# RoPE on one core: a zero word from each of 128 partitions between loads 0 and 1, and batch 0 stored whole

## The chip, the cores and the metric

The kernel runs on one core of a Trainium2 chip. Times are device microseconds of one launch; the time of a kernel is the median over its runs. A separate profiled execution gives the trace; its span is the time from the first to the last thing that the profile sees on the core.

## The reference

The input `x` has 8 batches of 2048 positions, 16 heads and 64 values, in float32. Each head's 64 values are two halves of 32, which are rotated by the position's 32 cosines and sines:

```python
out1 = x1 * cos - x2 * sin
out2 = x1 * sin + x2 * cos
return np.concatenate([out1, out2], axis=-1).astype(np.float32)
```

`x` and the output are 67.1 MB each, 8.39 MB a batch. There is no matrix product; three elementwise passes per batch are all of the arithmetic.

## The kernel before

**Tiling.** A batch has 2048 positions; partition p of the 128 holds positions 16p to 16p + 15, so a batch is 16 rows of 1024 values (J = 16) per partition, and a partition's share is one contiguous run of 64 KiB in `x` and in the output. On the chip the values are float16: `buf` (L47) holds NBUF = 5 batches, and batch b uses slot b mod 5, so batches 5, 6 and 7 reuse the slots of 0, 1 and 2.

**Transfers.** `load` (L62 to L71) and `store` (L73 to L81) issue one DMA each, from GpSimd. The transfer itself turns float32 into float16 on the way in and back on the way out. One DMA of a whole batch has 128 packets, one per partition, and 16 short completion packets of 4 bytes; a DMA of two batches has 256 and 16. All of these transfers stand in one queue, which is called the ring here: `in_ring` (L51 to L60) binds each one behind the one issued before it, so that GpSimd issues them in the order of the program and the queue serves them in that order.

SyncE issues four transfers on another queue: `sin_f` (L40), `head` (L41, the first two rows of batch 0 in float32, JA = 2), `cos_f` (L45), and at the end the last two rows of batch 7 (L135), which go out behind the ring's transfer called `gate` (L130).

**Compute.** `rotate` (L83 to L100) makes three VectorE passes over a batch: `v` = the swapped halves times the signed sines (L92), `buf` times the cosines in place (L98), and the sum in place (L100). ScalarE prepares the float16 tables (L104, L105, L110), turns `head` into float16 (L106), and turns the last two rows back (L134).

**Order.** Batch 0 is rotated in two parts, rows 0 and 1 (L111) and rows 2 to 15 (L115). The ring has, in order: load 0 without its first two rows (L102), load 1 (L103), the one-row store of batch 0 (L112), loads 2 and 3 in one DMA (L113), load 4 (L114), the other 15 rows of store 0 (L116), store 1, store 2, loads 5 and 6 (L121), load 7 (L122), stores 3 and 4 (L125), stores 5 and 6 (L128), and store 7 in two parts of 9 and 5 rows (L130, L131). The two-batch loads wait for the slots that they write over: L121 for stores 0 and 1, L122 for store 2. Loads 2 to 4 write slots that nothing has used; they wait for nothing but their place behind the one-row store, which waits for L111 and so for the cosines.

The constants that the program's start sets on GpSimd (zero and one in float32, and two others) are 128 x 1 tiles; the kernel before uses none of them in a transfer.

Of the kernel before, what the change touches and what calls it, by code (L numbers as in the profile page):

```python
# [1 line left out]

# [4 lines left out]


@with_exitstack  # L10
def kernel(
    ctx: ExitStack,
    tc: tile.TileContext,
    x: bass.AP,
    cos: bass.AP,
    sin: bass.AP,
    out: bass.AP,
):
    nc = tc.nc
    f16 = mybir.dt.float16  # L20
    f32 = mybir.dt.float32

    B, S, H, D = x.shape
    Dh = D // 2
    P = nc.NUM_PARTITIONS
    J = S // P
    NBUF = 5

    const_pool = ctx.enter_context(tc.tile_pool(name="rope_const", bufs=1))
    io_pool = ctx.enter_context(tc.tile_pool(name="rope_io", bufs=1))  # L30
    tmp_pool = ctx.enter_context(tc.tile_pool(name="rope_tmp", bufs=1))

    JA = 2
    head = const_pool.tile([P, JA, H, D], f32)
    x0 = x[0].rearrange("(p j) h d -> p j (h d)", j=J)
    sin_f = const_pool.tile([P, J, Dh], f32)
    cos_f = const_pool.tile([P, J, Dh], f32)
    cos_h = const_pool.tile([P, J, Dh], f16)
    sin_h = const_pool.tile([P, J, D], f16)
    nc.sync.dma_start(out=sin_f, in_=sin.rearrange("(p j) d -> p j d", j=J))  # L40
    nc.sync.dma_start(  # L41
        out=head.rearrange("p j h d -> p (j h d)"),
        in_=x0[:, 0:JA, :].rearrange("p j f -> p (j f)"),
    )
    nc.sync.dma_start(out=cos_f, in_=cos.rearrange("(p j) d -> p j d", j=J))  # L45

    buf = io_pool.tile([P, NBUF, J, H, D], f16)  # L47

    ring = []

    def in_ring(dma):  # L51
        if ring:
            tc.add_manual_dep(
                dma.ins,
                ring[-1].ins.name,
                mybir.DependencyInfo(mybir.DependencyClass.NoSync, mybir.DependencyReason.DATA),
                reason="order of the ring",
            )
        ring.append(dma)
        return dma  # L60

    def load(b, n=1):  # L62
        k = b % NBUF
        if n == 1:
            j0 = JA if b == 0 else 0
            dst = buf[:, k, j0:J, :, :].rearrange("p j h d -> p (j h d)")
            src = x[b].rearrange("(p j) h d -> p j (h d)", j=J)[:, j0:J, :].rearrange("p j f -> p (j f)")
        else:
            dst = buf[:, k : k + n, :, :, :].rearrange("p b j h d -> p b (j h d)")
            src = x[b : b + n].rearrange("b (p j) h d -> p b (j h d)", j=J)  # L70
        in_ring(nc.gpsimd.dma_start(out=dst, in_=src))  # L71

    def store(b, n=1, j0=0, j1=J):  # L73
        k = b % NBUF
        if n == 1:
            src = buf[:, k, j0:j1, :, :].rearrange("p j h d -> p (j h d)")
            dst = out[b].rearrange("(p j) h d -> p j (h d)", j=J)[:, j0:j1, :].rearrange("p j f -> p (j f)")
        else:
            src = buf[:, k : k + n, :, :, :].rearrange("p b j h d -> p b (j h d)")
            dst = out[b : b + n].rearrange("b (p j) h d -> p b (j h d)", j=J)  # L80
        return in_ring(nc.gpsimd.dma_start(out=dst, in_=src))  # L81

    def rotate(b, j0=0, j1=J):  # L83
        v = tmp_pool.tile([P, J, H, D], f16)
        n = j1 - j0
        js = slice(j0, j1)
        xt = buf[:, b % NBUF, js, :, :]
        shape = [P, n, H, 2, Dh]
        sin_b = sin_h[:, js, :].rearrange("p j (e d) -> p j e d", e=2).unsqueeze(2).to_broadcast(shape)
        cos_b = cos_h[:, js, :].unsqueeze(2).to_broadcast([P, n, 2 * H, Dh])  # L90
        xe = xt.rearrange("p j h (e d) -> p j h e d", e=2)
        nc.vector.tensor_mul(  # L92
            out=v[:, js, :, :].rearrange("p j h (e d) -> p j h e d", e=2),
            in0=xe[:, :, :, ::-1, :],
            in1=sin_b,
        )
        xw = xt.rearrange("p j h (e d) -> p j (h e) d", d=Dh)
        nc.vector.tensor_mul(out=xw, in0=xw, in1=cos_b)  # L98
        xa = xt.rearrange("p j h d -> p (j h d)")
        nc.vector.tensor_add(out=xa, in0=xa, in1=v[:, js, :, :].rearrange("p j h d -> p (j h d)"))  # L100

    load(0)  # L102
    load(1)  # L103
    nc.scalar.copy(out=sin_h[:, :, Dh:D], in_=sin_f)  # L104
    nc.scalar.mul(out=sin_h[:, :, 0:Dh], in_=sin_f, mul=-1.0)  # L105
    nc.scalar.copy(  # L106
        out=buf[:, 0, 0:JA, :, :].rearrange("p j h d -> p (j h d)"),
        in_=head.rearrange("p j h d -> p (j h d)"),
    )
    nc.scalar.copy(out=cos_h, in_=cos_f)  # L110
    rotate(0, 0, JA)  # L111
    store(0, 1, 0, 1)  # L112
    load(2, 2)  # L113
    load(4)  # L114
    rotate(0, JA, J)  # L115
    store(0, 1, 1, J)  # L116
    rotate(1)
    store(1)
    rotate(2)
    store(2)  # L120
    load(5, 2)  # L121
    load(7)  # L122
    rotate(3)
    rotate(4)
    store(3, 2)  # L125
    rotate(5)
    rotate(6)
    store(5, 2)  # L128
    rotate(7)
    gate = store(7, 1, 0, 9)  # L130
    store(7, 1, 9, J - JA)  # L131
    last = buf[:, 7 % NBUF, J - JA : J, :, :].rearrange("p j h d -> p (j h d)")
    dst = out[B - 1].rearrange("(p j) h d -> p j (h d)", j=J)[:, J - JA : J, :].rearrange("p j f -> p (j f)")
    nc.scalar.copy(out=head.rearrange("p j h d -> p (j h d)"), in_=last)  # L134
    end = nc.sync.dma_start(out=dst, in_=head.rearrange("p j h d -> p (j h d)"))  # L135
    tc.add_manual_dep(
        end.ins,
        gate.ins.name,
        mybir.DependencyInfo(mybir.DependencyClass.Sync, mybir.DependencyReason.DATA),
        reason="the last rows go out behind this part",  # L140
    )


# [1 line left out]
_INS = ['x', 'cos', 'sin']  # L145
_OUTS = [((8, 2048, 16, 64), 'float32')]


# [23 lines left out]
```

## Time and profile before

| what | us |
|---|---|
| median of 3 runs | 316.79 (316.6 to 317.02) |
| the profiled execution | 316.6 |
| its span | 314.8 |
| VectorE busy | 209.1 |
| one VectorE pass over a whole batch (7 of each line) | 8.69 |
| one VectorE pass over rows 2 to 15, over rows 0 and 1 | 7.63, 1.23 |
| GpSimd's issue of one transfer, mean of the stores | 0.586 |
| VectorE's wait for ScalarE's cosines (L98 for L110) | 15.5 |
| VectorE's wait for loads (L92), two times in all | 41.2 |
| GpSimd's wait for stores that free a slot (L71), two times in all | 48.9 |
| HBM read and written | 67.63 MB and 67.11 MB |

The page counts 3104 packets: 2528 on the ring's queue, which is 18 batch-wide parts of 128 rows and 14 sets of 16 completion packets, and 576 on SyncE's queue. Its rate in GB/s counts the bytes as they are written, so a stretch of loads (float16 on arrival) reads near 200 and a stretch of stores near 400 at the same pace of the engines. An engine's idle time is put down to what released it: what the page calls an unknown queue in the chain of waits is a landing that the chain doesn't follow further. Beside the page the trace keeps one record for each packet, with its queue, start, duration and bytes.

### The profile page before, as it was taken

The page shows a single profiled execution, that of the slowest core. Times are in us where ns is not written, and L with a number is a line of the kernel's source. Part 1 is how long each engine was busy: PE and PEld are TensorE (multiplying, and loading weights), DVE is VectorE, ACT ScalarE, POOL GpSimd, SP SyncE. Part 2 cuts the span into 40 slices and gives each one's busy share as a digit, 9 for nine tenths or more (in the row PEclk, how much of TensorE's full clock was granted, in tenths as well). Part 3 has the DMA queues.
Part 4 walks back from the last instruction along what each step waited for, and adds up shares of the span by engine and source line. Part 5 has one row for each costly group of instructions (what it writes and reads, how often), then busy time and mean ns, then how long its engine had stood idle before and what let it go on. Part 6 is the DMA issues. An engine that isn't in the chain of part 4 may idle for free.

```text
span 314.8 us, 115 instructions
## 1 busy us (share of the span) xinstructions
DVE 209.1 (66%) x27; ACT 6.8 (2%) x6; POOL 8.6 (3%) x18
## 2 busy tenths in 40 slices
DVE  0105999999499999999950000899999999910000
ACT  3200000000000000000000000000000000020000
POOL 1002000000000000000010000000000000010000
DMA  9899999999999899999999999999999999999998
GB/s 284 187 262 200 200 266 200 200 262 204 200 200 317 382 492 407 400 400 533 400 200 208 258 200 200 229 237 333 400 491 441 400 400 525 408 400 400 433 427 339
DMA packets 3104, 101.71 MB, mean 323 GB/s; under 512 B 288, under 2 KB 288, under 8 KB 672
## 3 DMA queue, kind: packets, MB, share of 16 engines
q0 software_dynamic: 2528, 99.09, 98.1%
q1 hardware_dynamic: 576, 2.62, 2.2%
HBM read 67.63 MB, written 67.11 MB: 428 GB/s over the span
## 4 chain that ended last, share of the span: by engine, by line
DVE 66%; another core or an unknown queue 13%; DMA 8%; ACT 1%; issue 0%; SPq 0%; DVEq 0%; ACTq 0%
DVE buf L98 22%; DVE buf L100 22%; DVE v L92 22%; DMA cos_f<-in_cos_dram 8%; ACT head L134 1%; ACT cos_h L110 0%; SPq L41 0%; SPq L40 0%; DVEq L92 0%; ACTq L134 0%
## 5 line engine op out<-in xcount | busy, mean ns | idle before, releaser
L92 DVE TENSOR_TENSOR v<-buf,sin_h 128x16384 f16<-128x16384 f16 (+2 forms) x9 | 69.7, 7744 | 51.4 <-DMA buf<-in_x_dram 41.2
L98 DVE TENSOR_TENSOR buf<-buf,cos_h 128x16384 f16<-128x16384 f16 (+2 forms) x9 | 69.7, 7744 | 15.8 <-ACT cos_h L110 15.5
L100 DVE TENSOR_TENSOR buf<-buf,v 128x16384 f16<-128x16384 f16 (+2 forms) x9 | 69.7, 7744 | 0.3
L81 POOL DMA_DIRECT2D out_dram<-buf x8 | 4.7, 586 | 219.4 <-DVE buf L100 219.4
L134 ACT CAST head<-buf 128x2048 f32<-128x2048 f16 x1 | 1.9, 1898 | 249.9 <-DVE buf L100 249.9
L71 POOL DMA_DIRECT2D buf<-in_x_dram x6 | 3.7, 628 | 49.7 <-DMA out_dram<-buf 48.9
L106 ACT CAST buf<-head 128x2048 f16<-128x2048 f32 x1 | 1.9, 1897 | 3.5 <-DMA head<-in_x_dram 3.5
L104 ACT ACT_TABLE_LOAD x1 | 1.3, 1283 | 0.7 <-PEq L156 0.7
L110 ACT CAST cos_h<-cos_f 128x512 f16<-128x512 f32 x1 | 0.6, 617 | 16.1 <-DMA cos_f<-in_cos_dram 16.1
L104 ACT CAST sin_h<-sin_f 128x512 f16<-128x512 f32 x1 | 0.6, 617 | 1.4 <-DMA sin_f<-in_sin_dram 1.4
L105 ACT ACTIVATE sin_h<-sin_f 128x512 f16<-128x512 f32 x1 | 0.6, 624 | 0.0
L156 POOL MEMSET const-float32-0.0<- 128x1 f32 x1 | 0.1, 100 | 0.2 <-issue 0.2
L156 POOL MEMSET const-bfloat16-1.0<- 128x1 bf16 x1 | 0.1, 103 | 0.0
L156 POOL MEMSET const-float32-1.0<- 128x1 f32 x1 | 0.1, 100 | 0.0
L156 POOL MEMSET const-uint8-127<- 128x1 uint8 x1 | 0.1, 100 | 0.0
## 6 DMA issues: line engine op xcount, KB each, us to landing
buf<-in_x_dram POOLq DMA_DIRECT2D x2, 8192.0 KB, 55.2
buf<-in_x_dram POOLq DMA_DIRECT2D x3, 4096.0 KB, 57.4
out_dram<-buf POOLq DMA_DIRECT2D x1, 7680.0 KB, 68.3
out_dram<-buf POOLq DMA_DIRECT2D x1, 4608.0 KB, 28.6
buf<-in_x_dram POOLq DMA_DIRECT2D x1, 3584.0 KB, 22.3
out_dram<-buf POOLq DMA_DIRECT2D x1, 2560.0 KB, 34.1
head<-in_x_dram SPq DMA_DIRECT2D x1, 1024.0 KB, 6.9
out_dram<-head SPq DMA_DIRECT2D x1, 1024.0 KB, 8.4
```

Of the source, the lines that this page charges most:

```text
L71: in_ring(nc.gpsimd.dma_start(out=dst, in_=src))
L81: return in_ring(nc.gpsimd.dma_start(out=dst, in_=src))
L92: nc.vector.tensor_mul(out=v[:, js, :, :].rearrange("p j h (e d) -> p j h e d", e=2), in0=xe[:, :, :, ::-1, :], in1=sin_b,)
L98: nc.vector.tensor_mul(out=xw, in0=xw, in1=cos_b)
L100: nc.vector.tensor_add(out=xa, in0=xa, in1=v[:, js, :, :].rearrange("p j h d -> p (j h d)"))
L104: nc.scalar.copy(out=sin_h[:, :, Dh:D], in_=sin_f)
L105: nc.scalar.mul(out=sin_h[:, :, 0:Dh], in_=sin_f, mul=-1.0)
L106: nc.scalar.copy(out=buf[:, 0, 0:JA, :, :].rearrange("p j h d -> p (j h d)"), in_=head.rearrange("p j h d -> p (j h d)"),)
L110: nc.scalar.copy(out=cos_h, in_=cos_f)
L134: nc.scalar.copy(out=head.rearrange("p j h d -> p (j h d)"), in_=last)
L156: nc = _bacc.Bacc("TRN2", target_bir_lowering=False, num_devices=1)
```

## The change

The one-row store of batch 0 goes. In its place, a DMA on the same queue and in the same order rule writes one float32 zero from each of 128 partitions of the constant tile to the first word of each partition's share of batch 0's output, 64 KiB apart; it stands between load 0 and load 1. Loads 2 to 4 are issued right behind load 1, ahead of the tables and the first rotation. Batch 0 is still rotated in two parts, and then stored in one DMA of 16 rows, which writes the zero words over.

```diff
     load(0)
+    first = out[0].rearrange("(p j) h d -> p (j h d)", j=J)[0:128, 0:1]
+    in_ring(nc.gpsimd.dma_start(out=first, in_=nc.const_aps.tensor(0.0, [128, 1], f32), allow_slow_non_contiguous=True))
     load(1)
+    load(2, 2)
+    load(4)
     nc.scalar.copy(out=sin_h[:, :, Dh:D], in_=sin_f)
...
     rotate(0, 0, JA)
-    store(0, 1, 0, 1)
-    load(2, 2)
-    load(4)
     rotate(0, JA, J)
-    store(0, 1, 1, J)
+    store(0)
     rotate(1)
     store(1)
```

## The prediction

> **What bounds the kernel now.** I read the page's summary by slices and by queues first, then the chain of waits, then the timeline of the queue that issues the transfers, then the issues with their landing times, and last the trace's record of each single DMA packet (queue, start, duration, bytes).
>
> ```profile
> DVE 209.1 (66%) x27; ACT 6.8 (2%) x6; POOL 8.6 (3%) x18
> DMA  9899999999999899999999999999999999999998
> q0 software_dynamic: 2528, 99.09, 98.1%
> ```
>
> The 16 DMA engines are busy in every slice, and q0, the queue that GpSimd fills (the ring), alone takes 98.1% of their time. DVE is busy for two thirds. The chain of waits still puts 66% on DVE:
>
> ```profile
> 78.40 4.89 another core or an unknown queue
> ...
> 161.88 36.10 another core or an unknown queue
> ...
> 276.66 1.90 ACT head L134
> ```
>
> That chain ends at 278.6 us, 36 us before the span does, and inside it DVE stands still for 4.89 and 36.10 us, each time until a load lands. So what ends last is the ring, not DVE. The timeline of GpSimd's queue shows how far ahead the ring is filled:
>
> ```profile
> 1.24 1.21 POOL L71 DMA_DIRECT2D buf<-in_x_dram  x2 [0.80 <-PEq L167]
> 29.53 0.54 POOL L81 DMA_DIRECT2D out_dram<-buf  x1 [27.08 <-DVE buf L100]
> 30.06 1.26 POOL L71 DMA_DIRECT2D buf<-in_x_dram  x2
> 52.52 0.54 POOL L81 DMA_DIRECT2D out_dram<-buf  x1 [21.19 <-DVE buf L100]
> 140.72 0.71 POOL L71 DMA_DIRECT2D buf<-in_x_dram  x1 [30.36 <-DMA out_dram<-buf]
> 159.97 0.56 POOL L71 DMA_DIRECT2D buf<-in_x_dram  x1 [18.54 <-DMA out_dram<-buf]
> 276.88 1.08 POOL L81 DMA_DIRECT2D out_dram<-buf  x2 [25.46 <-DVE buf L100]
> ```
>
> Against it I set the packet records, which give when each transfer's first packet starts on the first of the engines: load 0 5.28, load 1 22.97, the one-row store 42.71, loads 2 and 3 43.95, load 4 82.58, the rest of store 0 101.90, store 1 120.01, store 2 139.33, loads 5 and 6 158.64, load 7 197.27, stores 3 and 4 216.59, stores 5 and 6 255.20, the two parts of store 7 293.81 and 304.69, the last two rows 310.72. Each was issued long before its turn: the nearest misses are 13 us (issued 29.53, turn at 42.71), 18 us (140.72 for 158.64) and 17 us (276.88 for 293.81). No transfer ever waits for its issue, so the time is the sum of what the ring's transfers take, with 5.3 us ahead and 4 us behind.
>
> The records also give the price of a batch: a packet is one partition's row, each engine has eight of them, and they start 2.413 us apart (2.412 for stores): load 4 lasts 82.577 to 101.900 = 19.323 us, store 1 19.315. Only two stretches up to store 0 depart from that price. Load 1 lasts 22.966 to 42.705 = 19.739, that is **0.416 us above** load 4; its eighth packets took 2.74 to 2.90 us where the others took 2.43, right ahead of the first store of the program. And the one-row store (42.705 to 43.950 = 1.245) with the rest (101.900 to 120.011 = 18.111) make 19.356, **0.041 us above** one whole store.
>
> **The change, part by part.** All 16 batches' worth of rows still go through the same ring, so only these small terms can move.
>
> *The one-row store goes, store 0 leaves whole.* 19.356 becomes 19.315: -0.04 us. The ring has 14 transfers before and after (one store less, one word store more), so the 16 four-byte completion packets of a transfer (some 0.02 us per engine) cancel between them; I count the word store's +0.02 with its own price and the split's inside the 0.04.
>
> *Loads 2 to 4 move up by one store.* GpSimd issues them at about 3 to 4 us instead of at 30.06; their rows stand in the ring 38.6 + 19.3 us long wherever the one-row store is. Nothing runs dry either way (13 us of cover now). The ring then holds six transfers at once, 48 data packets per engine, where the trace shows 40 at most (at 162 us: loads 5 to 7 and stores 3 and 4). If it took fewer, GpSimd would wait with load 4 until load 0 had drained at 23.5 us; load 4's turn is at 82 us, and store 0 is not ready before about 50 us, so this costs nothing. Load 1 is issued one DMA instruction later, 1.91 + 0.54 = 2.45 us, for a turn at 22.97.
>
> *The wait that is added.* Store 0 writes the words again that the word store has written, so it waits for that landing, at about 24 us; it is issued near 50 us. Behind it on GpSimd stand store 1 and all later issues; none is delayed.
>
> *cos.* The other queue's transfers share the engines with the ring:
>
> ```profile
> sin_f<-in_sin_dram SPq DMA_DIRECT2D x1, 256.0 KB, 2.7
> cos_f<-in_cos_dram SPq DMA_DIRECT2D x1, 256.0 KB, 24.4
> out_dram<-buf POOLq DMA_DIRECT2D x1, 512.0 KB, 15.2
> ```
>
> cos's packets alternate with load 0's, and on 13 engines its last record comes behind load 1's first row, so it lands at 26.08. With short words there instead, it can land near 23.6, and DVE's first batch ends up to 2.4 us earlier. Worth nothing at the end: DVE then waits for load 2, 4.89 us now, and longer. Without that cover a late DVE would have 13 to 18 us of issue lead to use up first.
>
> *The word store's own price.* Each engine gets eight rows of 4 bytes, from a constant that the program has set at 0.24 us anyway, and a completion packet. No row of the trace writes 4 bytes to memory. From below: the cheapest 4-byte completion records take 0.009 us, so 8 x 0.009 = 0.07. From above: the first rows of sin, 2048 bytes met cold, took mostly 0.404 us where they were slow, so 8 x 0.404 = 3.2 us. Nearest in kind are the 4-byte records inside a stretch of stores, 0.042 us each: 8 x 0.042 = 0.34. The 2048-byte rows in flow, 0.081 us with some 0.075 of it for the bytes, also speak for the lower half. A gain from the words by themselves is excluded: they take ring time. I take 0.34 + 0.02 = +0.36.
>
> The Trainium skill, "DMA: Bandwidth & Descriptors" (section Specifications), speaks against small words: line rate needs 512 bytes or more, and below that an engine reads, modifies and writes. No store of before is that short (its shortest row has 4096 bytes), so no run here shows it yet; by the row above the sum below is +0.32 us, by that rule it is the third rival's +3.2.
>
> *The 0.416 us.* It is a stall at the turn from the first loads to the first store. No later turn from load to store has it (load 4 to store 0: the last packet took 2.432, load 7 to stores 3 and 4 the same). Either the first store of a program pays it, and then the word store pays it between loads 0 and 1 (0 net), or the short 4 KB rows caused it, and it goes (-0.416) or the shorter words cause it too (0). Worst, both the words and the first whole store pay: +0.416. I take 0: it moves.
>
> Sum: -0.04 + 0.36 + 0 = **+0.32 us**. The profiled execution took 316.6 (span 314.8, 1.8 around it), so such a one would take 316.9; the median of the runs, 316.79, is 0.19 above it, which gives **317.1**. A measurement of this kernel can tell about 0.2%, 0.63 us, from no change: the forecast is no change that can be told.
>
> **The rivals.**
> 1. *The stall goes with the 4 KB rows.* For it: its only place is ahead of them. Against: the first store is the same place. 317.1 - 0.42 = 316.7; with the cheapest words (0.07 for 0.34) 316.4. Still within 0.2%.
> 2. *Both turns stall.* For it: nothing but that the word store may be too short to clear whatever the first store meets. 317.1 + 0.42 = 317.5, just over the bound.
> 3. *The words go one at a time, each a round trip to memory* (the other side). Place: between loads 0 and 1 on every engine, so all of the ring behind moves. Price 8 x 0.404 + 0.02 - 0.04 = +3.2 us: 320.0. It decides from the point where a word costs more than (0.63 + 0.04 - 0.02) / 8 = 0.081 us, the price of a 2048-byte row in flow. For it: rows at the start of the kernel did wait 0.35 to 0.64 us each. Against: once the queue flowed, rows overlapped, and behind each store's completion packets the next transfer's rows begin 0.02 us later. The rule in the Trainium skill ("DMA: Bandwidth & Descriptors", Specifications) would amount to this.
> 4. *Doesn't do what it says: the words aren't spread.* All 128 on one engine, 128 x 0.042 = 5.4 us, and that engine ends last: 322. Against: the rows of every transfer in the trace start in sixteens, eight times per batch.
> 5. *Faster beyond the bound.* Load 1's start is also ragged: 22.966 comes 2.349 us after load 0's eighth packet where seven others came 2.204 apart, some 0.13 too much. If stall, split and raggedness all went and the words cost the least: -0.42 - 0.04 - 0.13 + 0.09 = -0.50, 316.3. It needs more that I don't see to pass 0.63.
>
> **How the numbers follow.** Forecast 0.45; rival 1 0.20, rival 2 0.08, rival 3 0.20, rival 4 0.03, rival 5 0.04. Faster by over 0.2%: rival 5 and a tail of rival 1, 0.04 + 0.03 = 0.07. Slower: most of rival 3 (0.18), 0.05 of rival 2, rival 4 = 0.26. Within: 0.67. The range goes from 316.3 (rivals 1 and 5) to 318.6, a word price of (318.6 - 316.79 + 0.02) / 8 = 0.23 us, about the middle of rival 3; left out are some 0.06 below, 0.10 of rival 3 and 0.03 of rival 4 above. The forecast's own range is 316.8 to 317.5.
>
> **What would show it.** In the changed profile: q0 still near 98% and no slice without DMA; load 1's first full rows some 0.4 us of words plus a stall after load 0's end; load 1 itself at 19.32 and load 4 to store 0 without a stall (if the stall is moved); cos landing near 24 us; 19.3 us for store 0; the chain with a longer wait for load 2. It is wrong if the ring shows a gap, if the words take over 0.65 us in all, or if the 2.41 us between rows changes anywhere.

## The result, and the profile after

The changed kernel takes 317.25 us (median of 15 runs, 317.06 to 317.78), the kernel before in the same sessions 316.62 (15 runs, 316.31 to 317.02): a ratio of 1.0022, with a 95% interval of 1.0015 to 1.0029. It is slower by 0.6 us. The profiled span goes from 314.836 to 315.579 us, +0.74.

The page of the changed kernel, the lines that answer to those shown of before:

```profile
span 315.6 us, 115 instructions
DVE 209.1 (66%) x27; ACT 6.8 (2%) x6; POOL 8.6 (3%) x18
DMA  9899999999999999999999999999999999999998
q0 software_dynamic: 2416, 99.09, 98.0%
```

Nothing of the kind of bound has changed. The ring has 112 packets fewer: the 128 words became 16 records of 32 bytes (as many as there are engines), where I had counted eight rows of 4 bytes on each engine. GpSimd's part of the timeline:

```profile
1.24 0.67 POOL L71 DMA_DIRECT2D buf<-in_x_dram  x1 [0.80 <-PEq L168]
1.91 0.54 POOL L104 DMA_DIRECT2D out_dram<-const-float32-0.0  x1
2.44 1.81 POOL L71 DMA_DIRECT2D buf<-in_x_dram  x3
50.26 0.54 POOL L81 DMA_DIRECT2D out_dram<-buf  x1 [46.01 <-DVE buf L100]
141.43 0.71 POOL L71 DMA_DIRECT2D buf<-in_x_dram  x1 [32.76 <-DMA out_dram<-buf]
277.65 1.08 POOL L81 DMA_DIRECT2D out_dram<-buf  x2 [25.46 <-DVE buf L100]
```

All five transfers are issued by 4.25 us, and store 0 at 50.26 for a turn at 101.39: the issues are as far ahead as before. In the chain of waits DVE starts earlier and then stands longer, 5.48 for 4.89 and 38.54 for 36.10 us:

```profile
76.14 5.48 another core or an unknown queue
...
160.21 38.54 another core or an unknown queue
...
277.43 1.90 ACT head L135
```

The 0.74 us lie in two places, and both are to be seen in the busy time by stretches. Its columns are the stretch, its length, the busy times of DVE, ACT and GpSimd, the clock, the share of the DMA engines and their GB/s; a packet counts in the stretch in which it starts. Each stretch lies between the last start of one set of 16 rows and the first start of the next, a few hundredths of a microsecond inside them, so in it no engine begins a row. Before, from load 1's last rows to the one-row store, and from load 4's last rows to store 0:

```profile
40.25:42.65 2.40, 2.40 (x1) 0.00 (x0) 0.00 (x0) 1.00 0.00 0
99.90:101.85 1.95, 1.92 (x2) 0.00 (x0) 0.00 (x0) 1.00 0.00 0
```

After, from load 1's last rows to load 2, and from load 4's last rows to store 0:

```profile
40.26:42.20 1.94, 1.94 (x1) 0.00 (x0) 0.00 (x0) 1.00 0.00 0
98.24:101.37 3.13, 3.10 (x2) 0.00 (x0) 0.00 (x0) 1.00 0.00 0
```

The stretch of an ordinary turn is 1.94 to 1.95 us long (the rows of one engine start 2.41 us apart, and the 16 engines start theirs over some 0.45 us). The turn into the first store of rows of 2 KB or more (called the first store of bulk below) was longer by 0.45 us before and is longer by 1.18 now. From the packet records, by the first of the 16 starts: load 1 begins at 22.896 where it was 22.966 (-0.070); it lasts 19.323 us for 19.739 (-0.416); the one-row store and the rest, 1.245 + 18.111, have become 19.315 (-0.041); loads 2 and 3 take +0.007; load 4 takes 20.536 for 19.323 (+1.213). That is +0.693 by the start of store 1, and from there every step equals that of before; the other 0.05 is that the last engine now runs 0.468 us behind the first, where it was 0.419.

So the turn that paid 0.38 us (2.817 between load 1's last packet and the one-row store, where 2.434 is the rule; the rest of load 1's 0.416 lies in its uneven rows) has not only moved: it pays 1.16 (3.590 between load 4's last packet and store 0). What sets its size is the question of the experiments. In what follows a stall is the step from the last packet of the transfer ahead to the first of the next, less 2.434 us, or less 2.22 us behind load 0, whose rows are shorter. Rows of the loads that start further apart than at this steady pace are called uneven. Each stall is read from one profiled execution.

### The profile page after: what moved, and what is told of

It reads as the page before. It is cut to its first block, busy times and chain, and to the rows that moved or that the text cites. A ratio compares the mean times of both kernels' runs of the same rounds, so it can differ in the third digit from the quotient of the medians.

```text
span 315.6 us, 115 instructions
## 1 busy us (share of the span) xinstructions
DVE 209.1 (66%) x27; ACT 6.8 (2%) x6; POOL 8.6 (3%) x18
## 4 chain that ended last, share of the span: by engine, by line
DVE 66%; another core or an unknown queue 14%; DMA 7%; ACT 1%; issue 0%; SPq 0%; DVEq 0%; ACTq 0%
DVE buf L98 22%; DVE buf L100 22%; DVE v L92 22%; DMA cos_f<-in_cos_dram 7%; ACT head L135 1%; ACT cos_h L114 0%; SPq L41 0%; SPq L40 0%; DVEq L92 0%; ACTq L135 0%
```

## The experiments

None of these kernels leaves work out: the words and the early rows that don't hold batch 0's final values are written over by store 0.

**The words taken away.**

```diff
-    first = out[0].rearrange("(p j) h d -> p (j h d)", j=J)[0:128, 0:1]
-    in_ring(nc.gpsimd.dma_start(out=first, in_=nc.const_aps.tensor(0.0, [128, 1], f32), allow_slow_non_contiguous=True))
```

> The changed kernel without its word store; the ring is load 0, load 1, loads 2 and 3, load 4, store 0. In the changed kernel the last packets of load 4 take 3.3 to 3.9 us, and the step from load 4's last packet to store 0's first is 3.590 us where 2.434 is the rule: a stall of 1.16 us; in the kernel before it was 0.41 us, ahead of the one-row store. Theory A (a stall at the turn to the first store of full rows that grows with the load time ahead of it; the words don't count): the stall stays 1.16, the span 315.5 within 0.1. Theory B (the words do it, by what they leave for store 0 to write over): the stall falls to 0.41 or less and the span to 314.8 or less. Theory C (the stall goes by the row size of the first store, 64 KiB against 4 KiB): 1.16. Theory D (the first transfer that is issued long after the ring started pays): 1.16.

317.29 us, a ratio of 1.0018 to the kernel before (1.0008 to 1.0028), span 315.39. The stretch ahead of store 0:

```profile
98.28:101.12 2.84, 2.81 (x2) 0.00 (x0) 0.00 (x0) 1.00 0.00 0
```

The stall is 0.92 us, the step from load 0's last packet to load 1 is 2.289 us, with the words 2.285. The words cost no ring time that could be told (with nothing between the two loads either, the kernel before has 2.349 us there and the kernel below that holds loads back 2.215) and don't cause the stall: theory B falls. That the stall is 0.92 and not 1.16 was not forecast.

**The one-row store behind load 4.** On top of the last edit, so without words:

```diff
     rotate(0, 0, JA)
+    store(0, 1, 0, 1)
     rotate(0, JA, J)
-    store(0)
+    store(0, 1, 1, J)
```

> No words; the one-row store is kept but stands behind load 4, and the other 15 rows right behind it. Theory A (grows with the load time ahead of the first store): 1.16 us of stall between load 4 and the one-row store, none behind it; span 315.5. Theory C (row size of the first store): 0.41 at the one-row store, span 314.8. Theory D (first transfer issued late): no forecast that differs from A or C.

One run, 317.74; span 315.97. The stretch ahead of the row:

```profile
98.60:101.50 2.90, 2.90 (x1) 0.00 (x0) 0.00 (x0) 1.00 0.00 0
```

The row waits 1.16 us (a step of 3.598 us). The stretch looks shorter because the last of the 16 engines began its last row of load 4 0.63 us behind the first. The rest of store 0, right behind the row, shows no stall of its own. So the length of the first store's rows does not set the stall (theory C falls), and theory A looked right. The span is longer than expected because rows of the loads were uneven too, by some 0.2 to 0.4 us together, a thing that comes back below.

**Rows of 4 KB between loads 0 and 1.**

```diff
     load(0)
+    first = out[0].rearrange("(p j) h d -> p (j h d)", j=J)[:, 0:H * D]
+    in_ring(nc.gpsimd.dma_start(out=first, in_=sin_h.rearrange("p j d -> p (j d)")))
     load(1)
```

(The two ScalarE instructions that fill `sin_h` stand ahead of it.)

> In place of the words, 128 rows of 4 KB are stored between loads 0 and 1, in float16 turned to float32 as the one-row store was, from the sine table (batch 0 is written over them later). Ring time of its own 1.25 us. Theory A: a stall of 0.41 x 17.6/37.4, some 0.2 us or less, between load 0 and these rows, and none between load 4 and store 0: span 315.58 - 1.16 + 1.25 + 0.2 = 315.9. Theory B: none between load 4 and store 0, or one as large as with the words. Theory C: 0.41 ahead of the rows and none later, 316.1. Theory D: none ahead of the rows (issued at some 5 us), 1.16 ahead of store 0, span 316.8.

317.80 in one run, span 316.04. The stretches ahead of the rows (a few packets of the cosine table fall into it) and ahead of store 0:

```profile
21.06:23.36 2.30, 0.00 (x0) 0.00 (x0) 0.00 (x0) 1.00 0.03 11
99.90:101.90 2.00, 1.97 (x2) 0.00 (x0) 0.00 (x0) 1.00 0.00 0
```

The stall ahead of the rows is 0.41 us, with 17.6 us of loads ahead of them where the kernel before had 37.4 and 0.38; between load 4 and store 0 there is none. The span is that of the kernel before with 1.25 us of ring time added, and 0.04 less for store 0 in one piece: 314.84 + 1.245 - 0.04 = 316.04. A stall that grows with the load time is not what this shows, so theory A loses its second half.

**Loads 2 to 4 held back by a wait, no early store.**

```diff
-    rotate(0, 0, JA)
-    store(0, 1, 0, 1)
-    load(2, 2)
+    begun = rotate(0, 0, JA)
+    held = load(2, 2)
+    tc.add_manual_dep(
+        held.ins,
+        begun.ins.name,
...
     load(4)
     rotate(0, JA, J)
-    store(0, 1, 1, J)
+    store(0)
```

(This is against the kernel before; `load` and `rotate` also return the instruction that they issue last.)

> No words and no one-row store; loads 2 to 4 are held back until the first two rows are rotated, as the one-row store held them in the kernel before, so a load is the first transfer that is issued late (some 28 us) instead of a store. Theory D (the first transfer issued late pays): 0.41 us between load 1 and load 2, none between load 4 and store 0, span 314.7. Theories A and C: no stall between load 1 and load 2, 1.16 between load 4 and store 0, span 315.5.

317.33 in one run, span 315.57; no stall between loads 1 and 2, 1.15 us ahead of store 0. The late issue of a transfer is not the cause: loads 2 and 3, issued late, pay nothing, and the first store pays.

**The one-row store between loads 3 and 4.** The order of the ring is then load 0, load 1, loads 2 and 3, the row, load 4, the rest of store 0.

```diff
     load(2, 2)
-    load(4)
...
     store(0, 1, 0, 1)
+    load(4)
```

> No words; the one-row store stands between loads 3 and 4, so that 77 us of loads are ahead of it and a load follows it, where the row behind load 4 (stall 1.16 us) had stores behind it and the rows behind load 0 and load 1 (0.41 us each) had loads. Theory F (what follows in the ring decides: 0.4 where loads follow, 1.16 where stores follow): 0.41 us ahead of the row, span 314.8. Theory G (the load time ahead decides, from about 40 us on): 0.8 to 1.1 us ahead of the row, none between load 4 and the rest of store 0, span 315.3 to 315.6.

316.72 in one run, span 314.96: the time of the kernel before (316.68 beside it). The stretch ahead of the row is hardly longer than the 2.40 us of before:

```profile
78.86:81.32 2.46, 0.00 (x0) 0.00 (x0) 0.35 (x1) 1.00 0.00 0
```

The stall is 0.46 us (a step of 2.893) with 77 us of loads ahead. Theory G has only a point between 77 and 96 us left; theory F, that what follows decides, fits.

**A word with a change of type.** The changed kernel with another source:

```diff
-    ... in_=nc.const_aps.tensor(0.0, [128, 1], f32) ...
+    ... in_=nc.const_aps.tensor(1.0, [128, 1], mybir.dt.bfloat16) ...
```

> The changed kernel with a bfloat16 one as the source of the word, so that the transfer turns it into float32 as the stores of batches do. Theory H (the first transfer that turns 16 bits into 32 pays): 0.2 to 0.4 us between load 0 and load 1, none between load 4 and store 0, span 314.4 to 314.9. Theory I (32 bytes an engine are too few to count, whatever their type): as in the changed kernel, none between loads 0 and 1, 0.9 to 1.2 between load 4 and store 0, span 315.4 to 315.6.

317.16 in one run, span 315.40. Ahead of store 0 the stall is 0.35 us, which neither theory named. But the rows of the loads are uneven here: from load 0's eighth packet to store 0 the ring takes 80.40 us where the rule gives 79.50 (2.22 for that packet, 32 x 2.413, three ends of 0.02). So 0.90 us were lost in all, 0.55 of them on the way (0.50 in loads 1 to 4), and the span is that of the kernel without words. Unlike the float32 words these went out as 128 records of 4 bytes, of some 0.02 us each, and load 0 to load 1 still took only 2.269 us. Theory H, which expected a faster kernel, falls.

**Rows of 2 KB of float32 between loads 0 and 1,** from `sin_f`:

```diff
+    first = out[0].rearrange("(p j) h d -> p (j h d)", j=J)[:, 0 : J * Dh]
+    in_ring(nc.gpsimd.dma_start(out=first, in_=sin_f.rearrange("p j d -> p (j d)")))
```

> In place of the words, 128 rows of 2 KB are stored between loads 0 and 1 from the float32 sine table, without a change of type; 0.65 us of ring time. Theory H (change of type): none ahead of the rows, 0.9 to 1.2 us between load 4 and store 0, span 315.9 to 316.2. Theory I (size): 0.41 us ahead of the rows, none later, span 315.4.

318.11 in one run, span 316.34. Two stalls: 0.54 us ahead of the rows and 0.34 ahead of store 0. Neither theory had that.

**The bfloat16 word ahead of load 0.**

```diff
+    first = ... [0:128, 0:1]
+    in_ring(... in_=nc.const_aps.tensor(1.0, [128, 1], mybir.dt.bfloat16) ...)
     load(0)
```

> The bfloat16 words again, but ahead of load 0, where the ring is empty. Theory H: what the first such transfer pays falls into the start, behind the sine table and the first rows that use the engines till 5.2 us anyway; no stall later, span 314.3 to 314.5, faster than the kernel before by 0.1 to 0.2%. Theory I: 0.9 to 1.2 us between load 4 and store 0, span 315.4 to 315.6.

317.54 us, a ratio of 1.0039 (1.0020 to 1.0057), span 315.55; 0.72 us ahead of store 0, and uneven load rows again (the largest step 0.18 us too long at 61.7 us). No gain; H is out.

**The row ahead of load 4's last row.** Load 4 in two parts, so that 95 us of loads are ahead of the one-row store and only 1.2 us of load behind it. Against the kernel with the row behind load 4 (`load` takes the rows as `store` does):

```diff
-    load(4)
+    load(4, 1, 0, J - 1)
...
     store(0, 1, 0, 1)
+    load(4, 1, J - 1, J)
```

> No words; load 4 is split: 15 of its rows, then the one-row store, then its last row, then the other 15 rows of store 0. So the one-row store has 95 us of loads ahead, nearly as many as the row behind load 4 (stall 1.16 us), but 1.2 us of load follows it. Theory F (what follows decides): 0.4 to 0.5 us ahead of the row, none ahead of store 0's rest, span 315.0. Theory F2 (the loads that follow must be long): 0.4 to 0.5 ahead of the row and more ahead of the rest of store 0. Theory G (load time ahead, from some point between 77 and 96 us): 0.9 to 1.2 ahead of the row, none later, span 315.6.

317.10 in one run, span 315.34. The stall ahead of the row is 0.39 us (2.669 where 2.28 is the rule for these rows), none ahead of the rest. By the stall theory G falls: with nearly the same loads ahead, 0.39 here and 1.16 behind load 4. But the span is above F's 315.0, because uneven rows of the loads lost 0.64 us on the way. With them 1.03 us went ahead of the row here, and 1.39 in the kernel with the row behind load 4 (0.23 of uneven rows). Whether uneven rows and stall are one loss is open, and with them a part of theory G for loads of over 77 us.

**Rows of 4 KB of float32 between loads 0 and 1,** from the rows in `head`:

```diff
+    first = out[0].rearrange("(p j) h d -> p (j h d)", j=J)[:, 0 : H * D]
+    in_ring(nc.gpsimd.dma_start(out=first, in_=head[:, 0, :, :].rearrange("p h d -> p (h d)")))
```

> In place of the words, 128 rows of 4 KB are stored between loads 0 and 1 without a change of type, from the first float32 rows of batch 0; as the 4 KB rows out of float16 (0.41 us ahead of them, none later) but for the type, and as the 2 KB rows of float32 (0.53 ahead of them, 0.34 ahead of store 0) but for the size. Size decides: 0.4 to 0.5 ahead of the rows, none ahead of store 0, span 316.0. The change of type decides: 0.4 to 0.5 ahead of the rows and 0.3 to 0.4 ahead of store 0, span 316.4.

318.59 in one run, span 316.82. The stretch ahead of the rows, and that ahead of store 0:

```profile
21.06:24.03 2.97, 0.00 (x0) 0.00 (x0) 0.00 (x0) 1.00 0.01 4
100.66:102.55 1.89, 1.86 (x2) 0.00 (x0) 0.00 (x0) 1.00 0.00 0
```

The stall is 1.09 us (a step of 3.306), at the place where the same bytes written out of float16 waited 0.41, and there is none later. No theory had that, and it fells F as well, since loads follow here. The two sets of rows also take the same ring time, 1.256 us here and 1.248 out of float16, so neither the bytes written nor the time that the store takes sets the stall. What differs is what the store reads: 8 rows x 2 KB = 16 KB an engine out of float16, 32 KB out of float32. That made the last theory, tried in the last run below. (The change of type differs too; the last run keeps it.)

**Rows of 512 bytes ahead of load 0,** from a zeroed float16 tile:

```diff
+    seed = const_pool.tile([P, 128], f16)
+    nc.vector.memset(seed, 0.0)
+    first = out[0].rearrange("(p j) h d -> p (j h d)", j=J)[:, 0:128]
+    in_ring(nc.gpsimd.dma_start(out=first, in_=seed))
     load(0)
```

> In place of the words, 128 rows of 512 bytes, out of float16, ahead of load 0, where the ring is empty and the first tables and rows still use the engines; own price 8 x (512 / 27200 + 0.006) = 0.2 us. If so short a store is enough to be the first store, no stall between load 4 and store 0, and what it pays itself falls beside the first rows: span 314.3 to 314.6, faster than the kernel before by 0.1%. If it is not: 0.3 to 1.2 us between load 4 and store 0, span 315.2 to 315.8.

317.39 us, a ratio of 1.0028 (1.0007 to 1.0049), span 315.48, with 0.78 us ahead of store 0. 2 KB read an engine are not enough to spare store 0 its stall.

**Two rows in the early store of the kernel before.**

```diff
-    store(0, 1, 0, 1)
+    store(0, 1, 0, 2)
...
-    store(0, 1, 1, J)
+    store(0, 1, 2, J)
```

> The kernel before with two rows in the early store of batch 0 in place of one (and 14 in the rest): 32 KB of float16 are read for it on each engine, where the one row has 16 KB (stall 0.41 us) and the float32 rows of 4 KB had 32 KB (1.08). Theory J (the stall grows with the bytes that the first store reads, up to some 32 KB an engine): 1.0 to 1.2 us ahead of the two rows, none ahead of the rest, span 315.4 to 315.6. Theory K (a short store out of float16 that loads follow pays 0.41, the float32 source was the difference): 0.41, span 314.8.

317.21 us (10 runs, 316.89 to 317.55) against 316.53, a ratio of 1.0021 (1.0011 to 1.0031); span 315.53. The stretch ahead of the two rows, where the kernel before has 2.40, and that ahead of the rest of store 0:

```profile
40.30:43.20 2.90, 2.90 (x1) 0.00 (x0) 0.00 (x0) 1.00 0.00 0
101.80:103.60 1.80, 1.77 (x2) 0.00 (x0) 0.00 (x0) 1.00 0.00 0
```

The stall is 1.01 us (3.442 less 2.434). The order of the ring, the issues and the total bytes are those of the kernel before; one row more in the early store brings the whole loss of the change back. Theory J had 1.0 to 1.2 and a span of 315.4 to 315.6, theory K 0.41 and 314.8: J holds. And the size fits an estimate: an engine moves 65536 bytes (counted in float32) in 2.412 us, 27.2 KB a microsecond. If it reads the first store's source at that pace, the 16 KB that the second row adds are 0.60 us, and the stall grew by 1.01 - 0.38 = 0.63.

**All of it together.** What the first store of bulk reads on each engine until a load stands behind it, its stall, and what uneven rows ahead of it lost besides:

| kernel | read an engine | stall, us | uneven rows of loads 1 to 4, us |
|---|---|---|---|
| before: one row behind load 1 | 16 KB | 0.38 | 0.03 |
| rows of 4 KB out of float16 behind load 0 | 16 KB | 0.41 | none ahead |
| one row between loads 3 and 4 | 16 KB | 0.46 | 0.00 |
| one row ahead of load 4's last row | 16 KB | 0.39 | 0.64 |
| 2 KB rows of float32 behind load 0 | 16 KB | 0.54, and 0.34 later | none ahead |
| two rows behind load 1 | 32 KB | 1.01 | 0.00 |
| 4 KB rows of float32 behind load 0 | 32 KB | 1.09 | none ahead |
| one row with the rest right behind it | 256 KB | 1.16 | 0.23 |
| changed: store 0 whole | 256 KB | 1.16 | 0.06 |
| no words; loads held back | 256 KB | 0.92; 1.15 | 0.00; 0.00 |
| bfloat16 words behind load 0; ahead of it | 256 KB | 0.35; 0.72 | 0.50; 0.38 |
| 512-byte rows ahead of load 0 | 256 KB | 0.78 | 0.12 |

Where the loads' rows were even, the stall follows the bytes up to about 32 KB and not beyond; the two kernels that read 256 KB with no store of any kind ahead have 0.92 and 1.15, so differences of 0.2 us say little. By 27.2 KB a microsecond 16 KB are 0.60 us and 32 KB 1.21; the stalls of these two sizes lie 0.1 to 0.2 under these. That the engines read the first store's source ahead while the last load's writes stand still is the reading that fits; the trace has no record of the reading side, so it is argued and not shown. That it befalls only the first store of bulk is shown: no later turn from load to store in any of these kernels has it, but for the second stall behind the 2 KB rows of float32. (From load 7 to store 3 the step is 2.434 or 2.435 us in every kernel.)

What stays open: why these 2 KB rows left 0.34 us for store 0, where 16 KB out of float16 left nothing; why the rows of the loads are uneven in some runs, and why bfloat16 words and 512-byte rows go with smaller stalls; and whether a first store that reads between 2 and 16 KB an engine would be cheaper, which wasn't tried. No kernel here beats the kernel before; the row between loads 3 and 4 equals it, in one run.

## Why the prediction was right or wrong

The time, 317.25, lies in the range (316.3 to 318.6) and close to the forecast of 317.1, and the direction was the forecast's: +0.63 us of median where +0.32 was expected. That it came so close is luck, as the terms below show. And "no change that can be told" did not hold: the interval of the ratio, 1.0015 to 1.0029, leaves 1 out. By its own steps:

- **The bound.** Right: the ring is never dry, every issue has a lead, and DVE's earlier start (cosines used at 24.50 us instead of 26.75) went into a longer wait for load 2.
- **Store 0 whole, -0.04.** Measured -0.041.
- **Loads 2 to 4 issued early, the added wait, cos.** All at nothing, as said: 98.0% of the queue, no turn without its transfer. (The ring held five transfers at once, which are six batch-wide parts with the words counted as one.)
- **The words, +0.36.** Mis-sized: they were 16 records of 0.013 to 0.015 us, and with or without them load 0 to load 1 takes 2.285 or 2.289 us. They cost nothing that could be told. The rule of the Trainium skill ("DMA: Bandwidth & Descriptors", Specifications), that below 512 bytes an engine reads, modifies and writes, may hold, but costs nothing to be seen here. The third rival, one round trip to memory for each word at +3.2 us, did not happen, and neither did the fourth, all words on one engine.
- **The 0.416 us, taken as "It moves", 0.** This is the step that failed. I saw the stall as the price of the first store or of short rows, and took it to be as large wherever it went. It moved and grew, from 0.38 to 1.16 us, or by the whole lengths of loads 1 to 4 +0.80 (1.213 + 0.007 - 0.416). The words drew no stall, and store 0 reads 16 times what the one row read. None of my cases had a stall that grows with the store; of the rivals, rival 2, with a second stall of 0.42, came nearest in time (317.5), for another reason.
- **The signs that were named.** Load 1 at 19.32, cos near 24 us (23.82), 19.3 for store 0 and q0 near 98% came. The stall and the words between loads 0 and 1 did not, nor a load 4 without a stall; and the rows of load 4 start up to 2.433 us apart instead of 2.413.

So +0.32 came near the measured time by errors that partly cancel: the words too dear by 0.36, and load 1 beginning 0.07 earlier besides, which I had left to a rival; the stall too cheap by 0.80. 0.32 - 0.36 - 0.07 + 0.80 = 0.69, the +0.693 of the records above.

## What to carry to other kernels

When transfers alone set the time, add up the records of single packets against their steady pace: the departures, here some 0.4 us in 315, were what this change of order could move, and each needs a cause of its own before it is carried along in a sum. Ask what a stall is proportional to (time ahead, rows, bytes read or written) before taking it to move unchanged. Where a ring begins with loads, a short first store with loads right behind it was worth 0.6 us here (ratio 1.0018 without it), and a row more in it lost that again (1.0021).

## What the runs showed of the hardware

- The first store of bulk on the ring held up the last load ahead of it by 0.38 to 0.54 us at 16 KB read an engine and by 0.92 to 1.16 at 32 KB and more (less, 0.35 to 0.78, in the three kernels with 16-bit words or 512-byte rows ahead); in the kernel before and after the change, the later turns from load to store had none.
- Ahead of that store the loads' rows are uneven now and then (steps up to 0.18 us too long); behind it the steps of the kernel before and after the change are the same 2.413 us for loads and 2.412 for stores to the end.
- 128 words of 4 bytes, 64 KiB apart in memory, went out as 16 records of 32 bytes of about 0.015 us and cost no ring time that could be told; from a bfloat16 source they went out as 128 records of 4 bytes, of some 0.02 us each.
